# Latents' norm factors as rows of 512, two operands of the first token block stored and loaded again, and queries on 512 columns, in a fused transformer layer on one core

## The chip, the core and the metric

The kernel runs on one core of one Trainium2 chip. The core has a matrix engine (TensorE, PE in the profile; its weight loads are PEld), a vector engine (VectorE, DVE), a scalar engine (ScalarE, ACT), a general engine (GpSimd, POOL) and a queue engine (SyncE, SP) that issues the transfers (DMA). Each engine takes its instructions in the order in which they were built and waits at each for what it needs; the engines run beside one another. The metric is the device time of the whole program in microseconds (us), from the first to the last instruction and the little that lies around them; lower is better.

## The reference, cut to what matters

One layer of a bidirectional encoder over 2048 tokens of 1024 features, fp32. Around the change lie the common input projection, the split into columns, and the latents of the attention, c_q (256 columns) and c_kv (128 columns), with their norms.

```python
def rms_norm(x, g):
    xf = x.astype(jnp.float32)
    y = xf * lax.rsqrt(jnp.mean(xf * xf, axis=-1, keepdims=True) + EPS)
    return (y * g.astype(jnp.float32)).astype(x.dtype)
...
def mla_group(c_q, c_kv, k_rope_pre, q_norm_g, w_uq, kv_norm_g, w_ukv, cos, sin):
    bsz, s, _ = c_q.shape
    q = (rms_norm(c_q, q_norm_g) @ w_uq).reshape(bsz, s, MLA_HEADS, QK_NOPE + QK_ROPE)
    q_nope, q_rope = q[..., :QK_NOPE], q[..., QK_NOPE:]
    q_rope = apply_rope(q_rope, cos[:, None, :], sin[:, None, :])
    kv = (rms_norm(c_kv, kv_norm_g) @ w_ukv).reshape(bsz, s, MLA_HEADS, QK_NOPE + V_HEAD)
...
    xn = rms_norm(h, ln_mix_g[l])
    proj = xn @ w_in[l]
    y_a = mlstm_group(...)      # columns q, k, v, o, gates of proj
    y_b = mla_group(...)        # columns c_q, c_kv, k_rope of proj
    h = h + jnp.concatenate([y_a, y_b], axis=-1) @ w_out[l]
    h = h + conv_gated_mlp(...)
    h = h + gate * rms_norm(p[l] @ w_ple_proj[l], ple_post_g[l])
return rms_norm(h, final_g)
```

## The kernel before, in words

The program runs through five stages: in_proj (the value columns v, 0 to 105 us), pairs (all other columns of the input projection, 105 to 436), queries (the attention's queries and values, 436 to 495), attention and mLSTM, and last the output projection, the gated MLP and the closing steps. Products are made with operands that `split` cuts into a high and a low part: a cast on ACT (L125) and a subtraction on DVE (L128), and three matmuls for each product (high by low, low by high, high by high).

**in_proj.** For each of 16 token tiles `nat` makes a product in one of four banks of the accumulator memory, and `vals` writes it out times the token's norm factor, a column of `rcol`. The factors come from `square_x` for tiles 0 to 7 and from `square` for tiles 8 to 15: the squares' sum for one tile, then `rsq` on POOL, which multiplies and adds (L146) and takes the power -1/2 (L148, the operation `pow` with the constant tile `nhalf`). `norm_row` turns eight columns of factors into a row with a matmul by the identity (L323), copies it and stores it.

**pairs.** Sixteen steps, i = 0 to 15: eight pairs of column blocks (j) for each of two blocks of 1024 tokens. Each step is one multiplication of 2 by 2 blocks in Strassen's manner (Winograd's form): seven products fx, fy, fz (L512, 12 matmuls of 128x512 each) out of sums of the weights' blocks (`pair_prep`, on DVE at L455 to L460) and of the tokens' blocks (B11, T1, T2, B21, T3, T4, B22). Two of a step's products, `rest_y` and `rest_z`, are made in the next step. The tokens' operands of block 0 come from `token_sums` during in_proj: all but B22 stay on chip in two parts, B22 goes to memory (`store_op`) and comes back in step 1 (`load`). The operands of block 1 are made by `next_sums` on the side in steps 1 to 5: it loads pieces of x (xsq, L405), scales them on DVE (L410), adds (L416 to L430) and stores the results (xo_d, L391). `pair_load` loads the weights of step i + 2 (fwr, L335).

The first two pairs of each block hold the latents. `conv` stores a latent (lat_d, L527) and squares it (lsq). In the third and fourth steps of each block, `sums` adds the squares over the features with eight matmuls that have one column each (L586), copies 128x8 sums (L588), and `rsq` makes the factors, again 128x8; `norm_row` at the seventh place of the step turns and stores them (lr_d, L326). The steps' side work stands in `side(at)`, at = 1 to 7 within a step. `rescale` later loads latents and factors and stores the scaled latents (rest_d).

**queries.** Eight column groups of 256 tokens. `rope` makes the rotated part with the latent as the stationary operand and turns it back by four transposes (L876) a group; `latent` makes the rest.

**The order of the work.** A scheduler places the instructions of DVE, ACT, POOL and SP; PE's order in queries is that of the code. All transfers are issued on SP's one queue: an entry whose wait isn't over holds all behind it. The constant buffers w7 and w11 hold the squares, t0 to t3 the xsq pieces, in turn.

Of the kernel before, what the change touches and what calls it, by code (L numbers as in the profile page):

```python
# [60 lines left out]
class Block:  # L61
# [4 lines left out]
    def __init__(self, ctx, tc, d):  # L66
# [13 lines left out]
        self.gt = self.cst.tile([P, 16, 16], F32, name="gt")  # L80
        self.raw, self.ops, self.p1tag = {}, {}, None
# [6 lines left out]
        self.q_d = dt([NH, 8, P, 2, 256], F32, name="q_d")  # L88
# [102 lines left out]
    def in_proj(self):  # L191
# [33 lines left out]
        def square(st):  # L225
            t = self.at(next(rows), [P, D], name="x_row")
            nc.sync.dma_start(t, d["x"][0, st * P:(st + 1) * P, :])
            sq = self.stat(1, "nt_s")
            nc.scalar.activation(t, t, AF.Square, accum_out=sq)
            self.rsq(sq, 1, 1.0 / D, rcol[:, st:st + 1])  # L230

        def square_x(st):

            t = self.at(next(rows), [P, KT, P], name="x_sq")
            nc.scalar.activation(t, xq[st], AF.Square)
            n = KT
            while n > 1:
                n //= 2
                nc.vector.tensor_tensor(t[:, 0:n], t[:, 0:n], t[:, n:2 * n], op=ALU.add)
            ps = self.tbank([P, 1])  # L240
            nc.tensor.matmul(ps, t[:, 0], self.nhalf[:, 0:1], start=True, stop=True)
            m = self.stat(1, "nt_m")
            nc.vector.tensor_scalar(m, ps, -2.0 / D, EPS, op0=ALU.mult, op1=ALU.add)
            nc.gpsimd.tensor_tensor(rcol[:, st:st + 1], m, self.nhalf[:, 0:1], op=ALU.pow)
# [44 lines left out]
        square_x(0)  # L289
        vals(0, first)  # L290
        work = chain(self.token_sums(), self.pair_begin())
        for st in range(1, NT):
# [14 lines left out]
            if st < 5:  # L307
                for q in range(2 * st - 1, min(2 * st + 1, 8)):
                    square_x(q)
# [37 lines left out]
    def token_sums(self):  # L347
# [20 lines left out]
        for k in range(4):  # L368
# [105 lines left out]
    def pairs(self):  # L474
# [41 lines left out]
        def conv(s, half):  # L516
            u = s.u[half]
            ts = slice(2 * SB * s.blk, 2 * SB * (s.blk + 1))
            if s.pr < 0:
# [10 lines left out]
                if s.pr == -1 and not half:  # L530
                    tt(sq, sq, s.sq[1], op=ALU.add)
# [50 lines left out]
        def sums(s, bank):  # L582

            ps = bank[:, 0:8]
            for t in range(8):
                nc.tensor.matmul(ps[:, t:t + 1], s.sq[0][:, t * P:(t + 1) * P], self.nhalf[:, 0:1], start=True, stop=True)  # L586
# [10 lines left out]
        for i in range(N):  # L597
# [10 lines left out]
            def side(at):  # L608
# [88 lines left out]
    def rescale(self, blk):  # L697

        nc = self.nc
        for n, h in ((0, 0), (0, 1), (1, 0), (1, 1)):  # L700
            ts = slice((2 * blk + h) * SB, (2 * blk + h + 1) * SB)
            row = self.row_bcast(self.at("t7", [P, SB], name="rrow"), self.lr_d[n][ts], SB)
            raw = []
            for k, e in enumerate((0, 1) if n else (2,)):
                t = self.at(f"t{4 + (h + k) % 2}", [P, SB], name="rsp")
                nc.sync.dma_start(t, self.lat_d[e, :, ts])
                raw.append((t, e))
            yield from pause(3)
            for t, e in raw:
                nc.vector.scalar_tensor_tensor(t, t, self.lgain[:, e:e + 1], row, op0=ALU.mult, op1=ALU.mult)  # L710
                nc.sync.dma_start(self.rest_d[:, e, ts], t)
            yield
# [19 lines left out]
    def queries_load(self):  # L732
# [8 lines left out]
        for kt in range(2):  # L741
            r = self.at(("w12", "w13")[kt], [P, 768], name="wqr")
            nc.sync.dma_start(r, d["w_uq"][0, kt * P:(kt + 1) * P, :])
            self.wqr.append(r)
# [7 lines left out]
    def queries_begin(self, at, bank):  # L752

        nc = self.nc
        if at in (2, 4):
# [14 lines left out]
        if at == 5:  # L770
            self.wo = [self.split_wo(0)]
            self.qcs = self.at("x7", [P, 8, 2, 64], name="qcs")
            for e in range(2):
                nc.sync.dma_start(self.qcs[:, :, e], self.d["rope"].rearrange("(c t p) a b -> t p c (a b)", t=2, p=P)[e])
        if at == 6:
            self.kh, self.kl = self.split_latent(0, ("x12", "x13"))

    def load_latent(self, c):

        raw = self.at(f"t{c % 2}", [P, 2, 256], name="qraw")  # L780
        self.nc.sync.dma_start(raw, self.rest_d[:, 0:2, c * 256:(c + 1) * 256])
        return raw
# [17 lines left out]
    def queries(self):  # L800
# [11 lines left out]
        rw = lambda kt, i: wq[kt][i].rearrange("p (h c) -> p h c", h=NH)[:, :, P:192]  # L812
        cc, ro = {}, {}

        def split_c(c):
            t = cc[c] = self.at(("w10", "w2")[c % 2], [P, 2, 2, 256], F32R, "cq")
            self.split(self.raws[c], t[:, 0], t[:, 1])
            if c + 2 < 8:
                self.raws.append(self.load_latent(c + 2))
# [11 lines left out]
        def rope(c):  # L831
            t = cc[c]
            ps = (self.bank if c < 6 else self.gbank)([P, 2, NH, 64], "qpr")
            for e in range(2):
                ts = slice(e * P, (e + 1) * P)
                for kt in range(2):
                    self.mm3(ps[:, e], t[:, 0, kt, ts], t[:, 1, kt, ts], rw(kt, 0), rw(kt, 1), kt == 0, kt == 1)
            tt = self.at("t2", [P, 2, 2, NH, 32], name="qtt")
            o = ro[c] = self.at("t3", [P, 2, NH, 64], name="qro")
            for e in range(2):  # L840
                x1, x2 = ps[:, e, :, 0:32], ps[:, e, :, 32:64]
                cos = self.qcs[:, c, e, 0:32].unsqueeze(1).broadcast_to([P, NH, 32])
                sin = self.qcs[:, c, e, 32:64].unsqueeze(1).broadcast_to([P, NH, 32])
                for a, b, f, out, op in ((x1, x2, 0, o[:, e, :, 0:32], ALU.subtract), (x2, x1, 1, o[:, e, :, 32:64], ALU.add)):
                    nc.vector.scalar_tensor_tensor(tt[:, f, 0], a, ASCALE, cos, op0=ALU.mult, op1=ALU.mult)
                    nc.vector.scalar_tensor_tensor(tt[:, f, 1], b, ASCALE, sin, op0=ALU.mult, op1=ALU.mult)
                    nc.vector.tensor_tensor(out, tt[:, f, 0], tt[:, f, 1], op=op)
# [1574 lines left out]
```

## Time and profile before

| What | Value |
|---|---|
| median of 3 runs | 2855.71 us (2852.88 to 2856.72) |
| the profiled execution's own time | 2856.03 us |
| its span, first to last instruction | 2854.3 us |
| granted TensorE clock, mean | 0.998 |
| busy: PE, PEld | 2814.3 us (99%), 2353.7 us (82%) |
| busy: DVE, ACT, POOL | 2154.1 us (75%), 1584.4 us (56%), 215.6 us (8%) |
| mean transfer rate | 195 GB/s |

A row of the timeline gives start, duration, engine, line, operation, the tile written and the tiles read, the shape (partitions x elements), and in brackets the idle time before it and what ended it; xN stands for N instructions in a row. A row of groups gives busy time, mean ns of one and the idle time just before them. Line numbers are those of the kernel before; the change shifts them by 2 to 20 (L335 becomes L340, L391 L395, L405 L409, L410 L414, L455 L459, L456 L460, L512 L516, L138 L140, L148 L150).

### The profile page before, as it was taken

Reading aid. Unit: us, or ns where it says so; the run is one execution under the profiler, and the core shown is the slowest. Engines: PE = TensorE matmul, PEld = TensorE weight load, DVE = VectorE, ACT = ScalarE, POOL = GpSimd, SP = SyncE. Lnnn points to the kernel's source line nnn. Section 1 sums busy time; section 2 is a strip of 40 time slices with the busy share of each in tenths; the row PEclk is TensorE's granted clock in tenths of the full one; section 3 lists DMA queues with packets and bytes.
Section 4 is the critical chain, followed back from the end, with each engine's and each line's share of the span. In section 5 each row is a group of like instructions: output and inputs, shape, how many; then the busy total and the mean of one; then the engine's idle time right before and its main releaser. Section 6 shows DMA issues by size and latency. Waiting matters only on the chain.

```text
span 2854.3 us, 39812 instructions
## 1 busy us (share of the span) xinstructions
PE 2814.3 (99%) x13918; PEld 2353.7 (82%) x13918; DVE 2154.1 (75%) x3588; ACT 1584.4 (56%) x3017; POOL 215.6 (8%) x299
## 2 busy tenths in 40 slices
PE   9999999999999999999999999999999999999998
PEld 7778878888888888888888888888888788888787
DVE  6877677778777777877778777777778767676777
ACT  6447576555666566655655556655556333254665
POOL 3000000000000000044200000000000000011012
PEclk9999999999999999999999999999999999999999
DMA  9786668554433333478735544667776757586865
GB/s 273 230 259 193 206 201 251 176 174 128 138 129 110 100 113 102 151 242 280 251 140 198 172 170 167 195 204 227 239 239 207 234 191 237 173 266 200 290 200 164
DMA packets 447570, 557.71 MB, mean 195 GB/s; under 512 B 37156, under 2 KB 294248, under 8 KB 447368
## 3 DMA queue, kind: packets, MB, share of 16 engines
q1 hardware_dynamic: 447368, 555.16, 61.0%
q8 instruction: 110, 1.80, 0.3%
q14 instruction: 92, 0.75, 0.1%
HBM read 361.25 MB, written 193.81 MB: 194 GB/s over the span
## 4 chain that ended last, share of the span: by engine, by line
PE 79%; DVE 5%; DMA 4%; ACT 2%; issue 1%; SPq 0%; POOL 0%; POOLq 0%; ACTq 0%; DVEq 0%
PE fy L1768 22%; PE fz L1768 15%; PE fx L1768 14%; PE ppv L1307 4%; PE tb L1295 3%; PE ppv L1308 2%; PE bk L1230 2%; PE bk L1232 2%; PE bk L1233 2%; PE bk L1231 2%; PE bk L1234 2%; PE fs L138 2%; PE fy L512 1%; PE mb L1169 1%; PE mb L1074 1%
## 5 line engine op out<-in xcount | busy, mean ns | idle before, releaser
L1768 PE MATMUL fz<-op,fw 128*128 128x512 f32 x1968 | 478.0, 391 | 4.4 <-ACT fw L125 2.1
L1768 PE MATMUL fx<-op,fw 128*128 128x512 f32 x1968 | 475.9, 390 | 0.0
L1768 PE MATMUL fy<-op,fw 128*128 128x512 f32 x1968 | 475.0, 390 | 0.0
L1768 PEld LDWEIGHTS fz<-op,fw 128*128 128x128 f32 x1968 | 367.1, 188 | 82.7 <-ACT fw L125 3.0
L1768 PEld LDWEIGHTS fy<-op,fw 128*128 128x128 f32 x1968 | 368.6, 188 | 76.8 <-DVE xt L1753 0.3
L1768 PEld LDWEIGHTS fx<-op,fw 128*128 128x128 f32 x1968 | 368.1, 188 | 76.1
L125 ACT CAST pt<-tb 128x512 fp32r<-128x512 f32 x256 | 147.1, 587 | 213.2 <-PE tb L1295 212.7
L1768 PE MATMUL fy<-op,fwd 128*128 128x512 f32 (+1 forms) x984 | 237.7, 390 | 1.6 <-DVE fh L1753 1.5
L1768 PEld LDWEIGHTS fy<-op,fwd 128*128 128x128 f32 x984 | 182.6, 188 | 39.9 <-DVE fh L1753 2.2
L1235 DVE TENSOR_REDUCE mx<-bk 128x1 f32<-128x512 f32 x256 | 175.4, 686 | 51.2 <-PE bk L1234 49.2
L128 DVE TENSOR_TENSOR pt<-tb,pt 128x512 fp32r<-128x512 f32 x256 | 173.4, 687 | 35.1 <-ACT pt L125 33.0
L128 DVE TENSOR_TENSOR fw<-fwr,fw 128x1024 fp32r<-128x1024 f32 x136 | 165.8, 1222 | 41.1 <-ACT fw L125 40.9
L1307 PE MATMUL ppv<-pt,kv 128*128 128x512 f32 x512 | 189.0, 407 | 1.0 <-DVE pt L128 1.0
L1252 ACT ACTIVATE pe<-bk,nm 128x512 f32<-128x512 f32 x256 | 174.6, 698 | 17.8 <-DVE nm L1246 16.0
L125 ACT CAST fw<-fwr 128x1024 fp32r<-128x1024 f32 x136 | 142.5, 1053 | 53.7 <-DVE fwr L1742 20.8
L1295 PE MATMUL tb<-ident,pe 128*128 128x128 f32 x1024 | 151.0, 273 | 3.4 <-DVE pt L128 3.3
L125 ACT CAST op<-opr 128x512 fp32r<-128x512 f32 x197 | 115.5, 621 | 68.2 <-DMA opr<-tw_d 15.2
L128 DVE TENSOR_TENSOR op<-opr,op 128x512 fp32r<-128x512 f32 x197 | 129.8, 696 | 22.9 <-ACT op L125 22.4
L1308 PE MATMUL ppv<-pt,kv 128*128 128x256 f32 x512 | 144.7, 283 | 0.0
L1295 PEld LDWEIGHTS tb<-ident,pe 128*128 128x128 f32 x1024 | 122.5, 140 | 23.7 <-DVE pt L128 5.6
L125 ACT CAST fw<-hraw 128x1024 fp32r<-128x1024 f32 (+1 forms) x72 | 70.4, 983 | 114.7 <-PE fx L1768 59.0
L128 DVE TENSOR_TENSOR fwd<-fwr,fwd 128x512 fp32r<-128x512 f32 x60 | 41.5, 691 | 112.0 <-ACT fwd L125 111.5
(410 smaller groups left out, 5273.4 us busy)
## 6 DMA issues: line engine op xcount, KB each, us to landing
fwr<-in_w_up SPq DMA_DIRECT2D x66, 512.0 KB
fh<-h_d SPq DMA_DIRECT2D x48, 512.0 KB
h_d<-fh SPq DMA_DIRECT2D x48, 512.0 KB
s_d<-fwr SPq DMA_DIRECT2D x44, 512.0 KB
fws<-s_d SPq DMA_DIRECT2D x44, 512.0 KB
rw<-row_d SPq DMA_DIRECT2D x32, 512.0 KB
fwr<-in_w_in SPq DMA_DIRECT2D x30, 512.0 KB
tw_d<-tsum SPq DMA_DIRECT2D x60, 256.0 KB
```

Source lines behind the costliest of these rows:

```text
L125: nc.scalar.copy(hi, src)
L128: (sub or nc.vector).tensor_tensor(lo, src, _f(hi), op=ALU.subtract)
L138: mm = lambda *a, **k: self.nc.tensor.matmul(*a, **k, skip_group_check=more)
L1230: mm(ps, ql, kh[:, ks], start=True, stop=False)
L1231: mm(ps, qr, self.krl[:, ks], start=False, stop=False)
L1232: mm(ps, qh, kl[:, ks], start=False, stop=False)
L1235: nc.vector.tensor_reduce(s.mx[:, kb:kb + 1], ps, axis=AX.X, op=ALU.max)
L1252: nc.scalar.activation(s.pe[:, kb % 2], s.banks[kb], AF.Exp, bias=s.nm, accum_out=s.rs[:, kb:kb + 1])
L1295: nc.tensor.transpose(t[:, j, :], s.p[kb][:, j * P:(j + 1) * P], self.ident)
L1307: mm(w.ps, vh[:, ks], pts[kb][:, j], start=kt == 0, stop=False, skip_group_check=True)
L1308: mm(w.ps[:, 0], vl[:, ks], pts[kb][:, j, 0], start=False, stop=kt == NT - 1, skip_group_check=True)
L1768: nc.tensor.matmul(out, a[:, k * P:(k + 1) * P], parts[lo][:, cols], start=first, stop=lo == 1 and k == last, skip_group_check=more)
```

## The change

It has five parts.

1. The latents' sums. The squares are split into a high and a low part (`split_squares`: 8 casts on ACT and 8 subtractions on DVE, 128x512 each), and a matmul with a stationary tile of ones adds each part over the features: two of 512 columns for each half of a block's 1024 tokens, 16 in all, with the result in a row. DVE scales one row of it (1x512), POOL takes the power -1/2 of that row, in place, and the row is stored in lr_d. Eight rows in all. The 32 one-column matmuls, the copies, the 128x8 factors and their transposes are gone. `sums` stands at places 1 and 2 of the step, no longer at 3 and 7.
2. Queries are made on 512 tokens at a time with the weights as the stationary operand: 288 matmuls of 128x256 become 144 of 128x512, and the 32 transposes are gone. The rotation works on 128x512 tiles in the turned layout (16 operations for 64 of 128x128), with a table made for it. Queries load the unscaled latent c_q and the row of factors and scale it there (8 operations), so `rescale` handles only c_kv: 12 loads and 12 stores become 4 and 4.
3. Of block 0, B21 and T4 too are stored in `token_sums` and come back in step 0: 8 stores and 8 loads more.
4. The token factors in in_proj are taken in groups, of four in `square` and of two in `squares_x`. The second block's `norm_row` moves from step 0 to step 1 in the code.
5. `next_sums` is stepped at other places of steps 1 to 5.

The core of the diff:

```diff
         def square(st):
+
             t = self.at(next(rows), [P, D], name="x_row")
             nc.sync.dma_start(t, d["x"][0, st * P:(st + 1) * P, :])
-            sq = self.stat(1, "nt_s")
-            nc.scalar.activation(t, t, AF.Square, accum_out=sq)
-            self.rsq(sq, 1, 1.0 / D, rcol[:, st:st + 1])
...
+            if st % 4 == 0:
+                self.ssq = self.stat(4, "nt_s")
+            nc.scalar.activation(t, t, AF.Square, accum_out=self.ssq[:, st % 4:st % 4 + 1])
+            if st % 4 == 3:
+                self.rsq(self.ssq, 4, 1.0 / D, rcol[:, st - 3:st + 1])
...
-            yield
-            split("B21", k, b[:, L])
-            tt(b[:, L], b[:, L], a[:, H], op=ALU.subtract)
-            split("T4", k, b[:, L])
+            self.store_op(0, "B21", k, b[:, L])
+            tt(a[:, H], b[:, L], a[:, H], op=ALU.subtract)
+            self.store_op(0, "T4", k, a[:, H])
             yield
...
-                if s.pr == -1 and not half:
-                    tt(sq, sq, s.sq[1], op=ALU.add)
+                if not half:
+                    if s.pr == -1:
+                        tt(sq, sq, s.sq[1], op=ALU.add)
+                    split_squares(s, 0)
                 return
...
-        def sums(s, bank):
-
-            ps = bank[:, 0:8]
-            for t in range(8):
-                nc.tensor.matmul(ps[:, t:t + 1], s.sq[0][:, t * P:(t + 1) * P], self.nhalf[:, 0:1], start=True, stop=True)
-            ssq = self.stat(8, "lssq")
-            nc.vector.tensor_copy(ssq, ps)
-            s.rc = self.rsq(ssq, 8, -2.0 / (P if s.pr == -2 else 2 * P))
-
-        begin(0, ("B22",))
+        def split_squares(s, half):
+
+            src = s.sq[0][:, half * SB:half * SB + SB]
+            t = self.at("w11", [P, 2, SB], F32R, "lsh")
+            self.split(src, t[:, 0], t[:, 1])
+            s.parts = t
+
+        def sums(s, half, bank):
+
+            n = P if s.pr == -2 else 2 * P
+            ps = bank[0:8]
+            for e in range(2):
+                nc.tensor.matmul(ps, self.ones, s.parts[:, 1 - e], start=e == 0, stop=e == 1)
+            if not half:
+                split_squares(s, 1)
+            row = s.sq[0][0:1, half * SB:half * SB + SB]
+            nc.vector.tensor_scalar(row, ps[0:1], 1.0 / n, EPS, op0=ALU.mult, op1=ALU.add)
+            nc.gpsimd.tensor_tensor(row, row, self.nhalf[0:1, 0:1].broadcast_to([1, SB]), op=ALU.pow)
+            o = (2 * s.blk + half) * SB
+            nc.sync.dma_start(self.lr_d[s.pr + 2][o:o + SB].unsqueeze(0), row)
+
+        begin(0, ("B21", "T4", "B22"))
...
-                if i == 0 and at == 7:
+                if i == 0 and at in (2, 3):
+                    load("B21", range(2))
+                if i == 0 and at in (5, 6):
+                    load("T4", range(2))
+                if i == 1 and at == 3:
                     self.norm_row(bank[0:8, 0:P], self.rcol[:, 8:16], self.r_d, 1)
...
-                if j in (2, 3) and at == 3:
-                    sums(lat[j - 2], bank)
-                if j in (2, 3) and at == 7:
-                    self.norm_row(bank[0:8, 0:P], lat[j - 2].rc, self.lr_d[j - 2], blk)
-                if 0 < i < 6 and at % 2:
+                if j in (2, 3) and at in (1, 2):
+                    sums(lat[j - 2], at - 1, bank)
+                if (1, 4) < (i, at) < (6, 0) and at not in (3, 6):
                     next(ahead, None)
...
+        def product(ps, b, o):
+            hi, lo = cc[b]
+            for kt in range(2):
+                self.mm3(ps, wq[kt][0][:, o:o + P], wq[kt][1][:, o:o + P], hi[:, kt], lo[:, kt], kt == 0, kt == 1)
```

How the built order moves, first on SP at the first latent's factors, third step of block 0. A name in square brackets is what the entry waits for: DMAHW0 to 7 are earlier transfers, the others engines. Before:

```order
L335 DMA fwr<-in_w_in 128x8x128 [waits DMAHW0_49,DVE_49]
L326 DMA lr_d_95<-r_1438 8x128 [waits DMAHW1_49,Activation_49]
L391 DMA xo_d<-xsq 128x512 [waits DMAHW2_49,DVE_49]
L405 DMA xsq<-in_x_turned 128x512 [waits DMAHW5_49,DMAHW3_49]
L405 DMA xsq<-in_x_turned 128x512 [waits DMAHW4_49]
```

And now:

```order
L607 DMA lr_d_97<-lsq 1x512 [waits DMAHW7_49,Pool_49]
L395 DMA xo_d<-xsq 128x512 [waits DMAHW0_49]
L395 DMA xo_d<-xsq 128x512 [waits DMAHW1_49]
L409 DMA xsq<-in_x_turned 128x512 [waits DMAHW2_49]
L607 DMA lr_d_97<-lsq 1x512 [waits DMAHW3_49,Pool_49]
L409 DMA xsq<-in_x_turned 128x512 [waits DMAHW5_49,DMAHW4_49]
```

The store of the factors waited for ACT's copy; the two stores of rows wait for POOL, with loads of xsq behind each.

DVE at the same place. The xsq rows are next_sums', the fwd and fwr rows the next step's weights. Before:

```order
L588 COPY lssq<-fs 128x8 [waits PE_49]
L410 SCALAR_TENSOR_TENSOR xsq<-xsq,gcol,rrow 128x512 [waits DMAHW2_49]
L128 TENSOR_TENSOR fwd<-fwr,fwd 128x512 [waits Activation_49]
L455 TENSOR_TENSOR fwr<-fwr 128x512 [waits DVE_49]
L410 SCALAR_TENSOR_TENSOR xsq<-xsq,gcol,rrow 128x512 [waits DMAHW4_49,DMAHW0_49]
L456 TENSOR_TENSOR fwr<-fwr 128x512 [waits DVE_49]
```

And now:

```order
L604 TENSOR_SCALAR lsq<-fs 1x512 [waits DVE_49,PE_49]
L434 TENSOR_TENSOR xsq<-xsq,xsd 128x512 [waits DMAHW0_49]
L414 SCALAR_TENSOR_TENSOR xsq<-xsq,gcol,rrow 128x512 [waits DMAHW2_49,DMAHW1_49]
L130 TENSOR_TENSOR fwd<-fwr,fwd 128x512 [waits PE_49,Activation_49]
L459 TENSOR_TENSOR fwr<-fwr 128x512 [waits DVE_49]
L414 SCALAR_TENSOR_TENSOR xsq<-xsq,gcol,rrow 128x512 [waits DMAHW5_49,DMAHW4_49]
L460 TENSOR_TENSOR fwr<-fwr 128x512 [waits DVE_49]
```

The weights' sums still stand behind scalings that wait for loads of xsq, now the loads that stand behind the rows' stores on SP.

PE round the sums of the first latent, before and now (fw and fwd are the weights' operands, op the tokens'; lsq and lsh are the squares and their two parts). Before:

```order
L512 MATMUL fz<-op,fw_1217 128x512 x4
L512 MATMUL fz<-op,fw_1216 128x512 x4
L512 MATMUL fy<-op,fwd 128x512 x12
L586 MATMUL fs<-nhalf,lsq 128x1 x8
L512 MATMUL fy<-op,fw_1222 128x512 x4
L512 MATMUL fy<-op,fw_1223 128x512 x4
```

And now, the first fx being step 2's first product and the second step 3's:

```order
L516 MATMUL fx<-op,fw_1187 128x512 x12
L600 MATMUL fs<-lsh,ones 8x512 x2
L516 MATMUL fz<-op,fw_1195 128x512 x4
L516 MATMUL fz<-op,fw_1196 128x512 x4
L516 MATMUL fz<-op,fw_1195 128x512 x4
L600 MATMUL fs<-lsh,ones 8x512 x2
...
L516 MATMUL fx<-op,fw_1357 128x512 x12
L516 MATMUL fz<-op,fw_1365 128x512 x3
L600 MATMUL fs<-lsh,ones 8x512 x2
```

The sums stand two products earlier, in two pieces around the second product.

More of the change, by code (lines that the diff above doesn't have):

```diff
@@ L80, in __init__ @@
         self.gt = self.cst.tile([P, 16, 16], F32, name="gt")
+        self.ones = self.cst.tile([P, 8], F32R, name="ones")
+        nc.vector.tensor_scalar(self.ones, self.nhalf, -2.0, None, op0=ALU.mult)
         self.raw, self.ops, self.p1tag = {}, {}, None
@@ L227, in square, with squares_x @@
             nc.sync.dma_start(t, d["x"][0, st * P:(st + 1) * P, :])
-            sq = self.stat(1, "nt_s")
-            nc.scalar.activation(t, t, AF.Square, accum_out=sq)
-            self.rsq(sq, 1, 1.0 / D, rcol[:, st:st + 1])
[L232 to L244, printed above, removed]
+            if st % 4 == 0:
[3 more added lines that the diff above has]
+                self.rsq(self.ssq, 4, 1.0 / D, rcol[:, st - 3:st + 1])
+        def squares_x(sts):
+            m = self.stat(2, "nt_m")[:, 0:len(sts)]
+            for i, st in enumerate(sts):
+                t = self.at(next(rows), [P, KT, P], name="x_sq")
+                nc.scalar.activation(t, xq[st], AF.Square)
+                n = KT
+                while n > 1:
+                    n //= 2
+                    nc.vector.tensor_tensor(t[:, 0:n], t[:, 0:n], t[:, n:2 * n], op=ALU.add)
+                ps = self.tbank([P, 1])
+                nc.tensor.matmul(ps, t[:, 0], self.nhalf[:, 0:1], start=True, stop=True)
+                nc.vector.tensor_scalar(m[:, i:i + 1], ps, -2.0 / D, EPS, op0=ALU.mult, op1=ALU.add)
+            nc.gpsimd.tensor_tensor(rcol[:, sts[0]:sts[-1] + 1], m, self.nhalf[:, 0:len(sts)], op=ALU.pow)
         def nat(st, warm=0):
@@ L699, in rescale @@
         nc = self.nc
-        for n, h in ((0, 0), (0, 1), (1, 0), (1, 1)):
+        for h in range(2):
             ts = slice((2 * blk + h) * SB, (2 * blk + h + 1) * SB)
[L702 to L711, printed above, removed]
+            row = self.row_bcast(self.at("t7", [P, SB], name="rrow"), self.lr_d[0][ts], SB)
+            t = self.at(f"t{4 + h}", [P, SB], name="rsp")
+            nc.sync.dma_start(t, self.lat_d[2, :, ts])
+            yield from pause(6)
+            nc.vector.scalar_tensor_tensor(t, t, self.lgain[:, 2:3], row, op0=ALU.mult, op1=ALU.mult)
+            nc.sync.dma_start(self.rest_d[:, 2, ts], t)
             yield
@@ L810, in split_wq, with split_c @@
             self.wor[1] = self.load_wor(1)
[L812 to L819, printed above, removed]
+        cc = {}
+        def split_c(b):
+            if b:
+                t = self.at(("x9", "x8")[b % 2], [P, 2, 2, SB], F32R, "cq")
+                hi, lo = t[:, 0], t[:, 1]
+            else:
+                hi, lo = [self.at(w, [P, 2, SB], F32R, "cq0") for w in ("w10", "w0")]
+            raw = self.raws.pop(b)
+            for e in range(2):
+                nc.vector.scalar_tensor_tensor(raw[:, e], raw[:, e], self.lgain[:, e:e + 1], raw[:, 2], op0=ALU.mult, op1=ALU.mult)
+            self.split(raw[:, 0:2], hi, lo)
+            cc[b] = hi, lo
+            if b + 2 < 4:
+                self.load_latent(b + 2)
         def weights(h):
@@ L863, in values, with latent @@
+        def latent(b, h):
+            if h % 2 == 0:
+                self.qo = self.at(f"u{h // 2}", [P, 2, SB], name="qo")
+            ps = (self.bank if h % 2 and b < 3 else self.gbank)()
+            product(ps, b, h * P)
+            nc.scalar.activation(self.qo[:, h % 2], ps, AF.Copy, scale=ASCALE)
+            nc.sync.dma_start(self.q_d[h, 0, :, b * SB:(b + 1) * SB], self.qo[:, h % 2])
         def values(vv, n):
```

152 lines of the change are left out of this document (68 added, 84 removed).

## The prediction

> **What bounds the kernel now.** I read the page's busy times first, then its chain of waits, then the timeline of each engine round the places that the change touches.
>
> ```profile
> span 2854.3 us, 39812 instructions
> PE 2814.3 (99%) x13918; PEld 2353.7 (82%) x13918; DVE 2154.1 (75%) x3588; ACT 1584.4 (56%) x3017; POOL 215.6 (8%) x299
> PE 79%; DVE 5%; DMA 4%; ACT 2%; issue 1%; SPq 0%; POOL 0%; POOLq 0%; ACTq 0%; DVEq 0%
> ```
>
> TensorE (PE) works 2814.3 of 2854.3 us: 40 us idle in all. So a saving is worth what it takes off PE's own rows, and a new stall counts in full once PE runs out of work. POOL is busy 8% and 0% of the chain. That share says nothing on what POOL costs if its work grows, and the change gives it eight operations of a size it never had.
>
> **The row on POOL.** Before, a latent's 1024 sums lie as 128 partitions by 8 columns, and one `pow` on POOL makes the factors (L148). Afterwards they lie as one row on one partition, and `pow` runs on 1x512, eight times (after's L605). These are the `pow` rows of three widths; the columns are start, duration, engine, line, operation:
>
> ```profile
> 39.93 0.55 POOL L148 TENSOR_TENSOR rcol<-rsm,nhalf 128x1 f32<-128x1 f32 x1
> 654.08 1.02 POOL L148 TENSOR_TENSOR rsr<-rsm,nhalf 128x4 f32<-128x4 f32 x1
> 313.37 1.64 POOL L148 TENSOR_TENSOR rsr<-rsm,nhalf 128x8 f32<-128x8 f32 x1
> 339.03 2.08 POOL L148 TENSOR_TENSOR rsr<-rsm,nhalf 128x8 f32<-128x8 f32 x1
> ```
>
> From one column to four is +0.47, that is 0.157 us a column; from four to eight is +0.62, that is 0.155. It is a line: 0.39 us and 0.156 a column. On it 512 columns take 0.39 + 512 x 0.156 = 80.3 us. The last row, slower beside other traffic, is 1.27 times the third: 102 us bounds the price from above. The line does not tell what *idle partitions* save: all rows here fill 128. If POOL paid for elements and not for columns, one 16th part (its partitions taken in sixteens, an assumption) gives 0.39 + 512 x 0.156/16 = 5.4 us. The other neighbours are POOL operations of that width that are not `pow`:
>
> ```profile
> L2066 POOL TENSOR_SCALAR xt<-xt,rsr 128x512 f32<-128x512 f32 x32 | 56.9, 1788 | 35.4 <-DMA h_d<-xt 30.2 <-DMA xt<-in_x 4.1 <-DVE yr L2036 1.0
> L1146 POOL TENSOR_SCALAR_AFFINE_SELECT mk<-rw 128x512 f32<-128x512 f32 x32 | 27.0, 867 | 617.6 <-PE mb L1169 281.7 <-PE mb L1074 269.7 <-DVE mx L1235 66.3
> ```
>
> They bound it from below: 0.87 to 1.79 us. Between 0.87 and 102 I take 80.3, because the rows of the same operation lie on one line, and a 128x8 `pow` (1.64) already costs nearly what a 128x512 multiply does (1.79).
>
> The Trainium skill, page "GPSIMD Engine Reference", section 3.1 "Elementwise — side-by-side cycle accounting", speaks against me: it counts about 2.6 cycles an element of a partition at 1.2 GHz for a two-operand operation, an estimate of 1.1 us for 512, and by it the result would be that of the cheap rows below, 2846. The `pow` rows agree that the cost goes by columns and show 0.156 us for each.
>
> **Who waits for the row.** The store of each row (after's L607) stands on SP's one queue and waits for POOL, and SP issues in order. In the built order one row's store stands just ahead of the loads of next_sums (`xsq`), the other between two of them; before, the factors' store stood there with only a small wait. Before, at this place:
>
> ```profile
> 166.66 0.29 SPq L326 DMA_DIRECT2D lr_d<-r  x1
> 168.37 0.34 SPq L391 DMA_DIRECT2D xo_d<-xsq  x1
> 168.81 0.88 SPq L405 DMA_DIRECT2D xsq<-in_x_turned  x2
> 172.57 1.50 DVE L410 SCALAR_TENSOR_TENSOR xsq<-xsq,gcol,rrow 128x512 f32<-128x512 f32 x2 [3.11 <-DMA xsq<-in_x_turned]
> ```
>
> An `xsq` load takes 172.57 - 168.81 = 3.8 us to reach DVE (3.5 from a later point of its issue). Queued behind that DVE operation, in order, are the sums of the next pair's weights (L456), and PE's second product of that pair reads them. So a held SP stops DVE, and DVE stops PE.
>
> Block 0. PE's rows before, x12 being one product of 2.72 us from start to start:
>
> ```profile
> 144.34 2.88 PE L512 MATMUL fx<-op,fw 128*128 128x512 f32 x12
> 147.06 2.88 PE L512 MATMUL fz<-op,fw 128*128 128x512 f32 x12
> 152.50 1.84 PE L586 MATMUL fs<-nhalf,lsq 128*128 128x1 f32 x16
> 154.21 3.03 PE L512 MATMUL fy<-op,fw 128*128 128x512 f32 x12
> 165.23 0.27 PE L323 MATMUL fs<-ident,rsr 128*8 128x128 f32 x1
> 165.26 3.01 PE L512 MATMUL fx<-op,fw 128*128 128x512 f32 x12
> 168.10 2.88 PE L512 MATMUL fz<-op,fw 128*128 128x512 f32 x12
> 189.14 2.88 PE L512 MATMUL fz<-op,fw 128*128 128x512 f32 x12
> ```
>
> The changed order has the first row's sum behind the fx product that ends at 147.06. Two matmuls of 0.23 (2.72/12) and a small eviction of some 0.7 (estimate: half of the DVE row x2 above is 0.75) put the first `pow` at 148.3. Two of them end at 148.3 + 160.6 = 308.9. The load adds 3.5: 312.4. PE meanwhile has the seven products up to pair 3's second (row 168.10): 20 us. DVE then has some 12 to 15 instructions before the next latent's squares are split, and the 128x1024 ones among them take 1.2:
>
> ```profile
> L128 DVE TENSOR_TENSOR fw<-fwr,fw 128x1024 fp32r<-128x1024 f32 x136 | 165.8, 1222 | 41.1 <-ACT fw L125 40.9
> L125 ACT CAST fw<-fwr 128x1024 fp32r<-128x1024 f32 x136 | 142.5, 1053 | 53.7 <-DVE fwr L1742 20.8
> ```
>
> So 15 us: the third `pow` starts at 327.4, the fourth ends at 488, its load is there at 491.5, and 5 us of sum, cast (1.05), subtraction (1.22) and their hand-overs let PE go on at about 496. That is in pair 4's second product, which before reached this operand at 190 (row 189.14 and a third of a product). Block 0 adds 496 - 190 = **306 us**.
>
> Block 1 is built alike: the sum now stands behind the product of the first row here, and what waits behind the rows' stores are the weights of pairs 12 and 13, the key rotation's loads and the gates'.
>
> ```profile
> 308.24 2.88 PE L512 MATMUL fz<-op,fw 128*128 128x512 f32 x12
> 351.32 2.88 PE L512 MATMUL fz<-op,fw 128*128 128x512 f32 x12
> 213.59 4.61 PE L512 MATMUL fy<-op,fwd 128*128 128x512 f32 x12 [1.94 <-DVE uv L545]
> ```
>
> Four rows are 321 us, and loads and DVE work as in block 0 some 25: 346, against the 44 that PE had from 308.24 to 352.2. It adds **302 us**. The last row shows that a product behind 1.94 us of idle took 4.61 where 2.88 is usual: 1.7 a restart, four long stops, **+6**.
>
> **What the change saves.** PE's rows in queries, 24 groups of twelve 256-wide matmuls and eight of transposes:
>
> ```profile
> 437.88 1.60 PE L138 MATMUL qpr<-wq,cq 128*128 128x256 f32 x12
> 439.32 1.60 PE L138 MATMUL gb<-cq,wq 128*128 128x256 f32 x12
> 445.01 0.60 PE L876 MATMUL gb<-ident,qro 128*128 128x128 f32 x4
> 445.37 1.68 PE L138 MATMUL gb<-cq,wq 128*128 128x256 f32 x12
> 446.88 1.60 PE L138 MATMUL bk<-cq,wq 128*128 128x256 f32 x12
> ```
>
> 24 x 1.44 (437.88 to 439.32) = 34.6 becomes 12 x 2.72 = 32.6: -1.9. The eight transposes go: 8 x (0.36, 445.01 to 445.37, + 0.07 that the next group's 1.51 is longer) = -3.4. Together **-5.3**. The sums' own matmuls: a group took 1.71 (152.50 to 154.21) plus 0.14 in the next product (154.21 to 157.07 against 2.72) and 0.15 for the transposed factors (165.26 to 168.10 is 2.84), 2.0 in all; four 512-wide ones take 0.91. That is -4.4 over four groups, but only where no row is waited for. Rope's 64 operations of 128x128 become 16 of 128x512, and the latents are scaled there; that is DVE work beside a busy PE, taken as 0. B21 and T4 go out to memory and come back in pair 0 (8 loads more): they lie on SP ahead of their use and DVE has 25% free; 0, and if that cover fails, an operand late by a load, 3.8 us.
>
> The hand-over from in_proj to the pairs waits for the last token tile's factor:
>
> ```profile
> 109.67 1.71 POOL L146 TENSOR_SCALAR rsm<-nt_s 128x1 f32<-128x1 f32 x1 [37.71 <-ACT x_row L229]
> 112.06 0.27 PE L323 MATMUL fs<-ident,rcol 128*8 128x128 f32 x1 [4.28 <-POOL rcol L148]
> ```
>
> With groups of four, tiles 12 to 14 wait for tile 15 too, and `pow` is four wide (1.02 for 0.55). The built order still has this transpose behind the first fz. So the idle 4.28 may go (-4.3) or three evictions more come on top (+5 with the wider `pow`); I take 0.
>
> **Sum**, against the profiled execution's 2856.03 us (its span is 2854.3; the median of the runs is 2855.71, the same within 0.02%): 2856.03 + 306 + 302 + 6 - 5.3 = **3465 us**.
>
> **Rivals.** (1) *Cheap rows*: 1 to 2 us each, as the wide POOL rows have. Then the row's store waits less than before, nothing is held, and -5.3 - 4.4 = -9.7 gives **2846**. For it: the 128x512 rows. Against it: the slope. (2) *By elements*: 5.4 us a row. Two hold SP 10.8 us; 148.3 + 10.8 + 3.5 + 5 = 167.6, just where pair 3's second product stood (168.10). So about 6 us a row is the point from which waiting decides; up to it the cost is a stop of 1 to 2 us at each pair, or the +5 of the hand-over: about **2852**, the same as before. (3) *Rows at half the price* (40 us, if long rows run with less overhead a column than 8): per block 4 x 40 + 26 - 43.5 = 142, so 2856 - 5 + 285 = **3136**. That the two steps of width lie on one line speaks against it.
>
> **How the numbers follow.** My forecast 0.70; cheap rows 0.15; by elements 0.10; half price 0.05. The forecast's own range: 72 us a row takes 8 x 8 = 66 off, 93 adds 100, so 3390 to 3570. A measurement of this kernel tells about 0.2% (5.7 us) from no change. Faster holds the cheap rows and a third of the by-elements case: 0.18; within the bound the rest of that case: 0.07; slower 0.75. The forecast's range holds some eight tenths of its 0.70; so the whole range has to reach down to the cheap rows, 2842 to 3570.
>
> **What would show it.** Right: eight POOL rows of 1x512 near 80 us each, starting near 148, 228, 327 and 407; SP's next entries behind them at the end of each; PE idle in two stops of about 150 us in each block with DVE waiting for `xsq` loads (block 0); the time from queries' end on unchanged. If the rows take 1 to 5 us, my line is wrong beyond eight columns or on one partition, and everything but the -5.3 falls with it. If the rows are long but PE's stops are much shorter than 306 in a block, the queue held less than I read in the order. A restart that is slow shows as a long product behind each stop.

## The result, and the profile after

| | us |
|---|---|
| before, median of 4 | 2855.97 (2852.88 to 2856.72) |
| changed, median of 4 | 3496.95 (3492.22 to 3501.68) |
| ratio | 1.2249, 95% interval 1.2231 to 1.2267 |
| predicted | 3465, range 2842 to 3570 |

The change costs 641 us. The page of the changed kernel, its profiled execution (3497.78 us), stands against the first lines shown in the prediction:

```profile
span 3496.0 us, 39243 instructions
PE 2822.2 (81%) x13690; PEld 2343.3 (67%) x13690; DVE 2160.2 (62%) x3525; ACT 1585.9 (45%) x3017; POOL 844.3 (24%) x284
PE   8901019402079999999999999999999999999998
POOL 0298970798910000000002510000000000001102
PEclk9955559756589999999999999999999999999999
PE 65%; issue 5%; POOL 5%; DVE 4%; DMA 3%; ACT 1%; SPq 1%; ACTq 0%; POOLq 0%; DVEq 0%
```

PE's busy time is nearly what it was (2822 for 2814); its share fell from 99 to 81% because it stands still. The forty slices show where: four holes in PE in the first third, and POOL busy in each. POOL's busy time grew by 629 us. In the chain of waits POOL has 5% by name, far less than the holes' share, so the chain is not the view to go by here; the waits say it better. First POOL's new group (busy, mean ns), then the waits of PE, of SP and of DVE in the pairs, from 140 to 1074 us (total, times, longest):

```profile
L605 POOL TENSOR_TENSOR lsq<-lsq,nhalf 1x512 f32<-1x512 f32 x8 | 657.6, 82207 | 203.5 <-DVE lsq L604 186.3
```

```profile
PE fz L516 <- DVE ug L482: 616.9, 4, 156.1
PE fs L600 <- DVE lsh L130: 6.3, 3, 3.0
```

```profile
SPq L607 <- POOL lsq L605: 656.4, 8, 84.5
```

```profile
DVE xsq L414 <- DMA xsq<-in_x_turned: 237.8, 5, 156.2
DVE xsq L434 <- DMA xo_d<-xsq: 82.4, 2, 81.6
DVE rsk L742 <- DMA rsk<-kr_d: 82.3, 3, 78.1
DVE gtmp L981 <- DMA rest_d<-rsk: 81.2, 1, 81.2
DVE rsk L743 <- DMA rsk<-kr_d: 80.6, 1, 80.6
DVE gtmp L959 <- DMA gtmp<-gate_d: 75.4, 1, 75.4
```

From POOL over SP and DVE to PE it is one chain. POOL works 82.2 us on a row. SP's store of the row waits for it (656 us over eight rows). DVE waits for the transfers behind that store: in block 0 for pieces of x (xsq), in block 1 for the key rotation's (rsk, rest_d) and the gates' loads. PE waits for DVE. PE's row names DVE's `ug` as the releaser, the operation that adds the product made before into `ug`. At each of the four stops it ends 0.15 us before PE goes on (at the first 330.93 for 331.08). It is short (0.68 us), but it stands in DVE's order behind the load's scaling and the weights' sums (L460):

```profile
242.88 0.75 DVE L414 SCALAR_TENSOR_TENSOR xsq<-xsq,gcol,rrow 128x512 f32<-128x512 f32 x1 [1.26 <-DMA xsq<-in_x_turned]
243.55 0.68 DVE L130 TENSOR_TENSOR fwd<-fwr,fwd 128x512 fp32r<-128x512 f32 x1
244.27 0.69 DVE L459 TENSOR_TENSOR fwr<-fwr 128x512 f32<-128x512 f32 x1
323.92 0.75 DVE L414 SCALAR_TENSOR_TENSOR xsq<-xsq,gcol,rrow 128x512 f32<-128x512 f32 x1 [78.95 <-DMA xsq<-in_x_turned]
324.59 0.68 DVE L460 TENSOR_TENSOR fwr<-fwr 128x512 f32<-128x512 f32 x1
328.51 1.22 DVE L130 TENSOR_TENSOR fw<-fwr,fw 128x1024 fp32r<-128x1024 f32 x1
330.25 0.68 DVE L482 TENSOR_TENSOR ug<-ug,fz 128x512 f32<-128x512 f32 x1
```

PE at the same places as in the prediction (the four stops stand in brackets):

```profile
152.06 2.88 PE L516 MATMUL fx<-op,fw 128*128 128x512 f32 x12
331.08 1.62 PE L516 MATMUL fz<-op,fw 128*128 128x512 f32 x3 [156.09 <-DVE ug L482]
511.07 5.46 PE L516 MATMUL fz<-op,fw 128*128 128x512 f32 x12 [154.39 <-DVE ug L482]
807.54 1.19 PE L516 MATMUL fz<-op,fw 128*128 128x512 f32 x2 [155.22 <-DVE ug L482]
984.88 5.46 PE L516 MATMUL fz<-op,fw 128*128 128x512 f32 x12 [151.16 <-DVE ug L482]
1073.57 1.56 PE L140 MATMUL gb<-woa,uvs 128*128 128x512 f32 x6
```

With the starts of the same products before (144.34, 189.14, 351.32, and 436.48 for the first row of queries) the kernel is late by 7.7 at its third step, 321.9 behind the second stop, 633.6 behind the fourth, 637.1 at queries and 641.7 at the end (3496.0 - 2854.3).

### The profile page after: what moved, and what is told of

Its sections match the earlier page's. It is cut to its first block, busy times and chain, and to the rows that moved or that the text cites. A ratio compares the mean times of both kernels' runs of the same rounds, so it can differ in the third digit from the quotient of the medians.

```text
span 3496.0 us, 39243 instructions
## 1 busy us (share of the span) xinstructions
PE 2822.2 (81%) x13690; PEld 2343.3 (67%) x13690; DVE 2160.2 (62%) x3525; ACT 1585.9 (45%) x3017; POOL 844.3 (24%) x284
## 4 chain that ended last, share of the span: by engine, by line
PE 65%; issue 5%; POOL 5%; DVE 4%; DMA 3%; ACT 1%; SPq 1%; ACTq 0%; POOLq 0%; DVEq 0%
PE fy L1788 18%; PE fz L1788 12%; PE fx L1788 12%; POOL lsq L605 5%; PE ppv L1327 3%; PE tb L1315 3%; PE ppv L1328 1%; PE bk L1250 1%; PE bk L1253 1%; PE bk L1252 1%; PE bk L1254 1%; PE bk L1251 1%; PE fs L140 1%; PE fy L516 1%; PE mb L1189 1%
## 5 line engine op out<-in xcount | busy, mean ns | idle before, releaser
L605 POOL TENSOR_TENSOR lsq<-lsq,nhalf 1x512 f32<-1x512 f32 x8 | 657.6, 82207 | 203.5 <-DVE lsq L604 186.3
L516 PE MATMUL fz<-op,fw 128*128 128x512 f32 x384 | 105.5, 426 | 619.1 <-DVE ug L482 616.9
L516 PEld LDWEIGHTS fz<-op,fw 128*128 128x128 f32 x384 | 79.2, 208 | 639.5 <-issue 619.0
L1788 PE MATMUL fz<-op,fw 128*128 128x512 f32 x1968 | 478.1, 391 | 2.1 <-DVE ug L1773 1.3
L1788 PEld LDWEIGHTS fz<-op,fw 128*128 128x128 f32 x1968 | 367.1, 188 | 80.4 <-DVE fw L130 1.8
L1166 POOL TENSOR_SCALAR_AFFINE_SELECT mk<-rw 128x512 f32<-128x512 f32 x32 | 26.8, 861 | 624.2 <-PE mb L1189 282.1
L414 DVE SCALAR_TENSOR_TENSOR xsq<-xsq,gcol,rrow 128x512 f32<-128x512 f32 x16 | 11.5, 747 | 245.4 <-DMA xsq<-in_x_turned 237.8
L1315 PE MATMUL tb<-ident,pe 128*128 128x128 f32 x1024 | 151.6, 273 | 2.8 <-DVE pt L130 2.6
```

The source lines that it names most:

```text
L516: nc.tensor.matmul(out, a[:, k * P:(k + 1) * P], parts[lo], start=first, stop=lo == 1 and k == 3, skip_group_check=more)
L605: nc.gpsimd.tensor_tensor(row, row, self.nhalf[0:1, 0:1].broadcast_to([1, SB]), op=ALU.pow)
L1315: nc.tensor.transpose(t[:, j, :], s.p[kb][:, j * P:(j + 1) * P], self.ident)
L1788: nc.tensor.matmul(out, a[:, k * P:(k + 1) * P], parts[lo][:, cols], start=first, stop=lo == 1 and k == last, skip_group_check=more)
```

## The experiments

The theory: eight powers of 82 us on POOL are the loss; they reach PE through SP's queue; and their price goes by the columns of the row. The other parts cost some 12 us instead of saving 5. The runs of the kernel before beside each group of experiments had medians of 2851.7 to 2853.9, some 3 us below the 2855.97 beside the changed kernel; a difference to the changed kernel's 3497.0 is known no better than that. Runs 2, 4, 5 and 6 are one execution each.

**1. The row's part undone, all else kept.** `sums`, its places and `norm_row` as before; the edit, cut to the places:

```diff
-                if j in (2, 3) and at in (1, 2):
-                    sums(lat[j - 2], at - 1, bank)
+                if j in (2, 3) and at == 3:
+                    sums(lat[j - 2], bank)
+                if j in (2, 3) and at == 7:
+                    self.norm_row(bank[0:8, 0:P], lat[j - 2].rc, self.lr_d[j - 2], blk)
```

> The changed kernel with its first part undone: the latents' sums are again eight one-column matmuls, their factors 128x8 on POOL and transposes; parts 2 to 5 stay. Theory (eight rows of 82 us on POOL, whose stores hold SP's queue, make the loss): the four stops of 155 us go. What is left is the hand-over from in_proj to the pairs, 7.7 us late in the changed kernel by its third step's first product (152.06 against 144.34), and queries with the rest, 4.6 us longer there (641.7 more in all, 637.1 of it before queries): 2856 + 7.7 + 4.6 = 2868, range 2858 to 2876. Rival 1 (the prediction's terms for the other parts hold): hand-over 0, queries -5.3, 2851. Rival 2 (the stops come from the new places of next_sums or of the operands' loads): still above 3300.

Measured: 2868.2 (2864.4 to 2870.8) beside 2853.2, ratio 1.0048 (1.0035 to 1.0061). 629 us go with this part, and the four stops with them; parts 2 to 5 cost 15 us, with the sign opposite to the prediction's.

**2. The row's part alone, in the kernel before.**

> The kernel before with the first part alone: squares split, sums as rows, power on eight rows of 1x512; all other parts as before. Theory: 8 x 82.2 = 658 on POOL, less what PE has to do meanwhile (some 20 us for each of four pairs of rows), with loads and sums of DVE behind each: four stops of about 155, 2856 + 4 x 155 + 10 = 3486, range 3440 to 3530. Rival (part of the loss comes from where parts 3 and 5 put the loads behind the rows): clearly below 3440.

Measured: 3491.4, one execution. The part does it alone; the loss does not need the places at which parts 3 and 5 put the loads.

**3. The power made a multiplication.**

```diff
-            nc.gpsimd.tensor_tensor(row, row, self.nhalf[0:1, 0:1].broadcast_to([1, SB]), op=ALU.pow)
+            nc.gpsimd.tensor_tensor(row, row, self.nhalf[0:1, 0:1].broadcast_to([1, SB]), op=ALU.mult)
```

> The changed kernel with POOL's power on the eight rows of 1x512 made a multiplication by the same constant (the latents' norm factors are left out, all else is there). Theory (the price is the power's): a row takes about 1.8 us, as the 128x512 multiplications on POOL do, no store holds SP, and the time is that of the kernel with columns less the 4 us that the row's matmuls save: 2864, range 2853 to 2872. Rival (one partition, or the waits of the row's store whatever its length, are what costs): rows above 20 us, time above 2950.

Measured: 2862.4 (2861.6 to 2864.8) beside 2853.2, ratio 1.0031 (1.0019 to 1.0043). The row on one partition, its store and the wait are all still there; only the operation is another. Its summary by tile (ns: least, median, most):

```profile
L605 POOL TENSOR_TENSOR lsq<-lsq,nhalf x8: 1029/1454/2077, 154.9 to 338.8; 1x512 f32<-1x512 f32 x8
```

1.45 us for 82.2: the power costs 56 times a multiplication of the same shape. The time is also 5.8 below that of the columns. That is near the 4.4 that the prediction had for the sums' own matmuls, but the intervals of the two ratios overlap, and the two traces do not show it there: from the third step's first product to the first row of queries they take 287.8 us with the rows and 286.7 with the columns, and from that row to the end 2421.4 and 2431.2.

**4. Eight partitions in place of one.**

```diff
-            row = s.sq[0][0:1, half * SB:half * SB + SB]
-            nc.vector.tensor_scalar(row, ps[0:1], 1.0 / n, EPS, op0=ALU.mult, op1=ALU.add)
-            nc.gpsimd.tensor_tensor(row, row, self.nhalf[0:1, 0:1].broadcast_to([1, SB]), op=ALU.pow)
+            row = s.sq[0][0:8, half * SB:half * SB + SB]
+            nc.vector.tensor_scalar(row, ps[0:8], 1.0 / n, EPS, op0=ALU.mult, op1=ALU.add)
+            nc.gpsimd.tensor_tensor(row, row, self.nhalf[0:8, 0:1].broadcast_to([8, SB]), op=ALU.pow)
...
-            nc.sync.dma_start(self.lr_d[s.pr + 2][o:o + SB].unsqueeze(0), row)
+            nc.sync.dma_start(self.lr_d[s.pr + 2][o:o + SB].unsqueeze(0), row[0:1])
```

> The changed kernel with the row's scaling and power on 8 partitions of 512 columns in place of 1 (the sum's result has eight equal rows). Theory (the power costs 0.156 us a column, however many partitions): rows of 82 us again, time 3497, range 3480 to 3515. Rival (by elements, one after the other): 0.39 + 8 x 81.8 = 655 us a row, time above 7000. Rival between (some cost for each partition): rows of 90 to 300 us.

Measured: 3494.4, one execution. POOL's group in it:

```profile
L605 POOL TENSOR_TENSOR lsq<-lsq,nhalf 8x512 f32<-8x512 f32 x8 | 657.6, 82208 | 201.9 <-DVE lsq L604 184.9 <-DMA xo_d<-xsd 17.0
```

Eight times the elements take the same time, 82208 ns a row for 82207. So leaving 127 partitions empty saves nothing: the same number of factors, 512, laid out as 128x4 takes 1.02 us (the 128x4 row in the prediction).

**5. Half the width.**

```diff
-            nc.gpsimd.tensor_tensor(row, row, self.nhalf[0:1, 0:1].broadcast_to([1, SB]), op=ALU.pow)
+            nc.gpsimd.tensor_tensor(row[:, 0:256], row[:, 0:256], self.nhalf[0:1, 0:1].broadcast_to([1, 256]), op=ALU.pow)
```

> The changed kernel with the power on the first 256 of a row's 512 columns only (half of the latents' norm factors are left out). Theory (price by columns, each us of a row counts in full because PE has only some 20 us of work for each pair of rows): a row takes 0.39 + 256 x 0.16 = 41.3 us, 8 x 40.9 = 327 less, 3170, range 3145 to 3190; this is also the prediction's rival of half price, 3136 with its terms. Rival (part of each row is hidden elsewhere): less falls away, above 3190.

Measured: 3172.1, one execution. Two rows in POOL's timeline:

```profile
154.60 82.60 POOL L605 TENSOR_TENSOR lsq<-lsq,nhalf 1x256 f32<-1x256 f32 x2 [39.41 <-DVE lsq L604]
```

41.3 a row here, 41.4 on the mean of all eight. From 256 to 512 columns are 40.8 us, 0.159 a column; and 8 x 40.8 = 326, where the time fell by 325 (3497.0 - 3172.1): what a row costs counts in full.

**6. The rows' stores off SP's queue.**

```diff
-            nc.sync.dma_start(self.lr_d[s.pr + 2][o:o + SB].unsqueeze(0), row)
+            nc.gpsimd.dma_start(self.lr_d[s.pr + 2][o:o + SB].unsqueeze(0), row)
```

> The changed kernel with the rows' stores issued on POOL's own queue in place of SP's. Theory 1 (SP's queue is what passes POOL's 82 us on, and nothing else): SP runs on until the loads that need the factors; POOL's eight rows end some 658 us after 156, about 815, where queries would begin at 443: 2868 + 370 = 3240. Theory 2 (a second holder stands right behind: the rows lie in the buffer w7, and in the built order ACT's squares of the next latent, in the same buffer, wait for POOL and for the store): ACT stops where SP did, the four stops stay within 10 us, 3485, range 3440 to 3510.

Measured: 3475.1, one execution. SP no longer waits for POOL, and the time is 22 us less, of which 5 lie ahead of the first row (POOL starts it at 151.6 for 156.3), in code that is the same in both. The rest stays, by the second holder. ACT's and PE's waits from 140 to 860 us, which holds the first three stops (at the fourth ACT waits 151.8 for the same store and PE 150.8):

```profile
ACT lsq L533 <- DMA lr_d<-lsq: 305.2, 2, 152.9
ACT ct L553 <- DMA lr_d<-lsq: 150.5, 1, 150.5
```

```profile
PE fs L600 <- DVE lsh L130: 304.8, 3, 152.4
PE fy L516 <- DVE uv L551: 150.8, 1, 150.8
```

The row lies in w7, and the next squares (L533) or the next convolution (L553) in the same buffer wait until it is stored. So the prediction's path through SP is the one that is taken in the changed kernel, but taking it away alone buys 3% of the loss. Rows in buffers of their own, which would take away the second holder as well, were not tried.

**7 and 8. The 15 us of the other parts: the hand-over.** Run 1 reaches its third step's first product at 150.84, 6.5 late. Undone in it were the grouping of the token factors (part 4), or the storing of B21 and T4 (part 3; the edit below is cut, the loads in step 0 go too).

```diff
-            self.store_op(0, "B21", k, b[:, L])
-            tt(a[:, H], b[:, L], a[:, H], op=ALU.subtract)
-            self.store_op(0, "T4", k, a[:, H])
+            yield
+            split("B21", k, b[:, L])
+            tt(b[:, L], b[:, L], a[:, H], op=ALU.subtract)
+            split("T4", k, b[:, L])
```

> The kernel of the columns run (changed kernel without its first part, 2868) with the fourth part undone too: token factors again one tile at a time. What is asked is where the 6.5 us go by which that kernel reaches its third step's first product later than the kernel before (150.84 against 144.34). Theory S (the stores of B21 and T4 hold the buffers of x in token_sums, so DVE's splits of x come late, PE idles 7.6 in in_proj where it idled 4.3, and the operands come back late): no change, 2868, range 2864 to 2872. Theory G (the grouped factors come late): 2862.

> The kernel of the columns run (2868) with the third part undone too: B21 and T4 of block 0 stay on chip. Theory S (stores): 2862, range 2858 to 2865. Theory G (grouped factors): 2868.

Measured: 2864.6 (2861.5 to 2867.2) without the groups, 2864.9 (2862.1 to 2867.5) without the stores, beside 2853.3; the ratios are 1.0038 (1.0025 to 1.0050) and 1.0036 (1.0024 to 1.0049), where run 1 had 1.0048 (1.0035 to 1.0061). Both times lie just inside the ranges of theory S and 3 to 4 us below run 1, but the three intervals overlap, so the times decide nothing. In the traces the third step's first product starts at 146.69 and 145.57, with run 1's 150.84. One trace each is thin here too: in the five kernels with parts 3 and 4 as before (the kernel before, runs 2 and 9 to 11) it starts at 142.6 to 146.5, in the six with both as changed (the changed kernel, runs 1 and 3 to 6) at 147.3 to 152.1. The means are 5.7 apart, and undoing either part alone brings the start back near the first group. PE's largest waits in the kernel before, up to 520 us, then up to 160 us in run 1, without the groups, and without the stores:

```profile
PE bk L138 <- DVE xh L128: 4.3, 5, 1.4
PE fs L323 <- POOL rcol L148: 4.3, 1, 4.3
```

```profile
PE bk L140 <- DVE xh L130: 7.6, 5, 2.9
PE fs L328 <- POOL rcol L150: 2.6, 1, 2.6
PE fz L516 <- ACT fw L127: 1.4, 1, 1.4
```

```profile
PE bk L140 <- DVE xh L130: 5.8, 4, 2.3
PE fs L325 <- POOL rcol L150: 2.9, 1, 2.9
```

```profile
PE fs L328 <- POOL rcol L150: 5.1, 1, 5.1
PE bk L140 <- DVE xh L130: 4.0, 4, 1.4
```

With both parts, DVE's split of x in in_proj is what PE waits longest for, 7.6 us where the kernel before had 4.3 (5.2 to 7.4 in the five others with both parts). Why undoing either part helps about as much is left open.

**9 to 11. The 15 us: queries.** Part 2 alone in the kernel before; then with the second head's output weights loaded earlier; then with a buffer of its own for two of the copies `woo`. The edit of the second, cut to the load:

```diff
-            self.wor[1] = self.load_wor(1)
+            both = self.at("x10", [P, 2, 2, SB], name="qcs")
+            t = self.tables[b] = both[:, 0]
+            self.wor[1] = self.load_wor(1, both[:, 1].rearrange("p a t -> p (a t)"))
```

> The kernel before with the second part alone (queries on 512 tokens). Columns run: +15 against the kernel before beside it, of which 6.5 came before its third step; so queries cost about 8.5 there, where the prediction had -5.3. In that run PE waited 7.3 in queries for the second head's output weights (cast of woa on ACT, behind the load wor, issued at 441 in place of 426) and ran slowly behind it, and 4.4 for the first q_t. Theory (these waits belong to part 2: more loads for a group stand on SP's queue ahead of wor): 2853 + 8 = 2861, range 2856 to 2865. Rival (they came with the shift of the other parts): the matmuls saved show, 2848.

> The same with the second head's output weights (wor) loaded into the free half of the buffer x10, with the first rope table, in step 15's sixth place in place of queries' start. Theory (the late load is the wait): the 7.3 us and the slow rows behind it go, 2852 if only the 4.4 of q_t stays, 2848 if that goes too; range 2846 to 2855. Rival (queries are held by DVE's and ACT's work, whichever load comes first): 2858 or more.

> The kernel of the run before it (queries on 512 tokens, output weights loaded early; 2852.7 beside 2853.9) with a buffer of its own (w13) for the copies woo of the second and fourth head. In that run PE waited 3.0 + 0.8 in queries for ACT's copies woo, and ACT for the stores of the copies before (7.5 us), which stood on SP behind the stores of the rotated queries; with restarts some 5 us. Theory (the saving of 5.3 us in matmuls is there and was taken back by waits for buffers): 2848, range 2845 to 2852. Rival (the next wait, DVE's load of the rope table, 6.8 us there, holds the same place): 2853, as before.

Measured: 2865.1 beside 2853.9 (ratio 1.0037, 1.0023 to 1.0051); 2852.7 (2849.6 to 2857.2) beside the same (0.9997, 0.9989 to 1.0006); 2859.0 (2852.2 to 2866.9) beside 2851.7 (1.0029, 1.0017 to 1.0040). PE's largest waits up to 560 us in the first, the second and the third (whose profile is that of its fastest run, 2852.15):

```profile
PE bk L140 <- ACT woa L127: 6.9, 1, 6.9
PE bk L1232 <- DVE q_t L130: 4.4, 1, 4.4
```

```profile
PE fs L325 <- POOL rcol L150: 4.2, 1, 4.2
PE bk L140 <- DVE xh L130: 4.0, 3, 2.5
PE bk L140 <- ACT woo L846: 3.0, 1, 3.0
```

```profile
PE bk L1236 <- DVE q_t L130: 7.4, 1, 7.4
PE fs L325 <- POOL rcol L150: 4.2, 1, 4.2
```

The late load of the second head's output weights is the loss of part 2: moved, 12 us come back. PE at these weights, in the kernel before and in run 9:

```profile
436.48 1.56 PE L138 MATMUL gb<-woa,uvs 128*128 128x512 f32 x6
443.64 1.54 PE L138 MATMUL bk<-woa,uvs 128*128 128x512 f32 x6
```

```profile
433.18 1.56 PE L140 MATMUL gb<-woa,uvs 128*128 128x512 f32 x6
444.36 0.80 PE L140 MATMUL bk<-woa,uvs 128*128 128x512 f32 x1 [6.89 <-ACT woa L127]
```

Two things came together. PE now comes to them sooner: 4.3 us behind the first row of queries (437.47), with one product of 12 matmuls between, where the kernel before has four and 7.2 us. And the load is later: issued 3.5 us behind that row (436.63), after loads of the latent and two stores on SP's queue, where the kernel before issues it 0.2 ahead of it (436.26). The 426 that the expectation gives for the kernel before is the load of another head: the weights that came by it were split only at 444.70, behind PE's use at 443.64.

The forecast saving of 5.3 in matmuls does not show even so. The third run lies above both its theory and its rival. The trace kept of it is that of its fastest execution, 7 us below its median: in it the waits for `woo` are gone, as the theory said, and 7.4 us of waiting for the first `q_t`, a load of what queries have just stored, stand in their place; what makes its other executions longer no trace shows. No version here is faster than the kernel before; the second of these equals it.

## Why the prediction was right, and where it was off

- **The row's price**: 80.3 predicted, 82.2 measured. The line through 1, 4 and 8 columns held to 512; its slope was 0.156 and is 0.160. This is 15 us over eight rows. The rivals of cheap rows and of a price by elements are excluded by runs 3 and 4 (it is the power, and the partitions do not count), the half-price one by the price itself; but its sum (3136 at 40 us) is a fair forecast of run 5 (3172 at 41.3). The Trainium skill's figure ("GPSIMD Engine Reference", section 3.1), by which a row would take 1.1 us, is near the multiplication (1.03 at the least, 1.45 in the median) and not the power.
- **Where it waits**: at the forecast places, pair 3's second product and pair 4's, in both blocks, with DVE behind the xsq loads in block 0. What PE waits for there is not quite what the prediction said. It took the next pair's weights for the last to come; the last is DVE's `ug`, which stands behind them in DVE's order, so the held queue has the same effect. The first power was forecast for 148.3 and started at 156.3, of which 7.7 is the hand-over.
- **Block 0 and block 1**: 306 and 302 were forecast, and 6 for the restarts. Measured are 314 (321.9 - 7.7) and 312 (633.6 - 321.9), and 629.4 up to queries (637.1 - 7.7); with the 15 us for the rows' price the forecast's terms are 629. That they meet so closely is in part luck, by two misses of opposite sign: the next point, and the stretch before queries, named below.
- **Restarts**: +6 forecast, 1.7 each. Measured are 2.5 to 3.1 each, some 10 in all: behind the second and the fourth stop a product took 5.46 for 2.88, behind the other two a short wait cuts the product in two.
- **The step that failed: the parts costed at 0 or as a gain.** The hand-over was taken as 0, with +5 as the bad end, and was +7.7 in the profiled execution (5.7 between the means of the traces above). The factor named for it came little later: PE's wait for it was 4.7 for 4.3. Of the 7.7, 4.1 are there when in_proj ends (the first product of the pairs starts at 108.95 for 104.90), 2.9 of them longer waits for DVE's splits of x (7.2 for 4.3); the rest are waits of 1.4 and 0.8 for ACT and a slow product of 4.78 behind them. Queries and what follows were forecast at -5.3. From queries' first row to the end they came to +4.6 in the changed kernel (641.7 - 637.1) and to +13.4 in run 9 (2431.2 for 2417.8). The matmuls' saving is right by the rows, 12 groups of 2.72; not seen was how soon PE comes to the second head's weights and how late their load stands on SP's queue. The cover was looked for on PE and DVE, and not on SP's queue in that stage.
- **A gain without a term.** Run 9 costs 11 as a whole and not 13.4, because part 2 also shortens the stretch from the third step's first product to queries: 287.7 us in run 9 for 292.1 before, and 921.5 in the changed kernel for 927.8 in run 2, which lacks part 2. PE's waits in that stretch are 1.3 us in run 9 where the kernel before had 4.7. Why they go was not tested.
- **The sum**: 609 forecast, 641.7 measured. Of the 33 missing are 15 the rows' price, 8 the hand-over, 10 queries. The stated range holds this, but it reaches down to the cheap rows and so says little; its own ends are 9 and 5 us wider than the terms given for them (3465 - 66 and 3465 + 100). What carries the forecast is the row's price and the place of the stops.

## What to carry to other kernels

An operation's share of the time says nothing on what it costs in another shape: fit its price from the shapes in the trace, in columns, and multiply it out before a layout over 128 partitions is traded for a row. A few small results turned to lie along one partition can cost more than the transposes that they save; keep a power on POOL across the partitions, and price any other function from its rows first. And where an engine's result goes out by an in-order queue, list what is queued behind it, and then the next holder behind that (here a buffer), before you count on a gain from moving the first. When a product is moved forward in an engine's order, look up when its operands are loaded.

## What the runs showed of the hardware

POOL's power costs 0.16 us a column whether 1, 8 or 128 partitions hold data (82.2 us for 512 columns on 1 and on 8 partitions; 1.64 for 8 columns on 128), when a multiplication of 1x512 takes 1.45.

TensorE's granted clock falls in a stop and comes back late. The changed kernel in three stretches: the second stop, the 8 us behind it, and the 12 after (the columns are stretch, length, busy time of PE, PEld, DVE, ACT, POOL, granted clock, DMA share, GB/s):

```profile
358.00:510.00 152.00, 0.00 (x0) 0.00 (x0) 4.57 (x6) 2.94 (x3) 143.71 (x2) 0.50 0.05 16
510.00:518.00 8.00, 6.93 (x19) 5.49 (x20) 7.01 (x13) 3.62 (x7) 0.00 (x0) 0.60 1.01 318
518.00:530.00 12.00, 12.00 (x54) 9.95 (x53) 8.61 (x14) 7.40 (x10) 0.00 (x0) 1.00 0.69 198
```

0.50 in the stop, 0.60 on the mean of the next 8 us, then 1.00. In steps of 1 us, the clock falls about 3.5 us into the first stop (work ends at 175.0; 1.00 up to 178, 0.75 in the next step, then 0.50). It comes back some 5.3 us after work begins behind the second stop (511.07; 0.50 up to 516, 0.79 in the next step, then 1.00) and 6.0 us behind the fourth (984.88; 0.56 from 990 to 991). The Trainium skill, "TensorE: Matmul & The Clock Gate", Part 1, states that an idle array falls to half clock after about 3.4 us and is released after at least one window of about 3.4 us of work; the fall agrees, the release came later than that least time here. The stops are nearly the whole reason why the changed kernel's mean clock reads 0.906 for 0.998: an estimate from the waits, 617 us at half clock in a span of 3496.0, gives 0.088 of the 0.092. So the low mean is a result of the stops, and of the time it makes only the restarts' 10 us.
